# A hybrid decoder layer on one core: the order of one weight pair, and a new form of the last norm and its stores

## The chip, the cores and the metric

The kernel runs on one core of a Trainium2 chip. The metric is the device time of one execution in microseconds (us), the median over several runs. Before the change it is 730.70 us over three runs (730.41 to 731.08).

The core's engines work side by side, each through its own queue in order: TensorE (PE in the profile, with weight loads as PEld) multiplies into the eight PSUM banks, VectorE (DVE), ScalarE (ACT) and GpSimd (POOL) work element by element, and SyncE (SP) issues transfers, as ScalarE and GpSimd can too. An instruction waits on semaphores for the data or the buffer it needs, and everything behind it in its queue waits with it.

## The reference

One layer over x of 1024 tokens by 1024 channels. What matters here is its end:

```python
v = jax.nn.silu(layernorm(v, cln_g[l], cln_b[l]))
v = v @ pw2_w[l] + pw2_b[l]                       # 1024 x 1024, the pointwise projection
y_conv = v * jax.nn.silu(cs)
...
y = jnp.concatenate([y_conv, y_lru], axis=-1) @ w_out[l]
x = x + (1.0 + gate[:, None, :]) * y
return rmsnorm(x, final_g)                        # y * rsqrt(mean(x*x) + eps) * final_g
```

Ahead of it stand a modulated norm, a projection to 5120 channels, two depthwise convolutions, the gates and a linear recurrence. All is float32.

## The kernel before

Activations lie transposed: 128 channels on the partitions, tokens along the free dimension, eight channel tiles of 128 x 1024. A float32 product is made of three products of float32r operands, high x high, high x low, low x high, so each operand is split: ScalarE casts it to the high part, VectorE subtracts that to get the low part. A product of 128 x 512 outputs over half of the contraction (four k tiles) is twelve matmuls.

**The plan.** The program is written as a list of operations with an engine, an estimated cost, a priority (`prio`, lower first) and their operands. `Plan.order` runs a list scheduler over them and so fixes, for every engine, the order in which instructions stand in its queue. `after=` adds a predecessor for this plan only: it shapes the order and sets no semaphore. On the chip an instruction waits for its true operands and buffers alone.

**The pointwise projection `pw2`.** Its eight output tiles are made in four pairs (line 1363). A pair uses a scheme of seven block products (`pair_products`), whose first operations are kept as `ops[0]` to `ops[6]`. `pair_weights` (line 559) loads the pair's two weight tiles into two buffers of the pool `raw` (it has two), casts the first (`whi...`), casts half of the second (`hl...`), makes four combinations of halves in place with VectorE and splits those (`h12`, `l12`, `h34`, `l34`), in all two loads, four ScalarE casts and eight VectorE operations, with five tiles of the large pool (`big`, 47 buffers). The loads are planned after `last[:1]`, the first product of the pair before, and the combinations and the second cast after `last[1:]`, the fourth product of the pair before. The outputs `yc` are then split once more for the output projection (`quarters`, tiles `yh*`, `yl*`).

**The output projection.** Tile 6 first, then pairs (0, 1), (2, 3) and (4, 5); tile 7 (`OUT_Z`) runs beside the last pair. The accumulators are `fin0` to `fin7`, which start as the residual x plus the recurrent half's product. The last pair and tile 7 run over the columns in three pieces, `END` = 0 to 512, 512 to 768, 768 to 1024. For each piece `add` and `gated` add products into `fin`, and `squares` has ScalarE square them (`finsq`) and VectorE add the squares into `finss`; the squares of tile 7 go to a tile of their own, `finsqz`, in the second and third piece.

**The last norm, one call of `norm` (line 1429) a piece.** `rstd` (line 687) sums the square tiles over the partitions with TensorE, tile by tile (`finbc<-ones,finss`, then `finbc<-ones,finsqz`), takes the root on ScalarE (`sd`), the reciprocal on VectorE (`rs`), and spreads the result over the partitions with TensorE (`finbc<-ident,rs`). In the last piece it runs idle products as well (`warm_mm`, four ahead of the sums and two behind them, `WARM`), and a second spread into a bank `idle`. `norm` then copies the result to SBUF (`bc`, in every piece), and makes the eight outputs: VectorE multiplies `fin` by `final_g` and by the spread in one instruction; tiles 6 and 0 of the second and third piece, which ScalarE has scaled by `final_g` ahead, go to GpSimd. Each output has a store of its own, 256 KB in the first piece and 128 KB in the others, into `out[m*128:(m+1)*128, a:e]`, rows of 4 KB in DRAM of which 2 KB or 1 KB are written. SyncE issues them, ScalarE those of the tiles in `AP`.

Of the kernel before, what the change touches and what calls it, by code (L numbers as in the profile page):

```python
# [11 lines left out]
AF = mybir.ActivationFunctionType  # L12
ALU = mybir.AluOpType

P = 128
D = 1024
T = 1024
KT = D // P
# [19 lines left out]
END = ((0, H), (H, 768), (768, T))  # L38
# [18 lines left out]
WPW = ("DVE", "DVE", "DVE", "DVE")  # L57
WOUT = ("DVE", "DVE", "DVE")
WZ = "DVE"
AP = {0: (), 512: (1, 5), 768: (1, 3, 5, 7)}  # L60
NP = {0: (), 512: (6, 0), 768: (6, 0)}
SUMS = (2, 6, 1, 4, 3, 0, 7, 5)
QRES = 0
AHEAD = 4
IDLE, IDLE0 = 13, 4
WARM = (4, 2)
BEHIND = 2.6
Z0 = 0.6
ROOTP = 57
# [226 lines left out]
def hymba_layer(ctx: ExitStack, tc: tile.TileContext, xT, vecs, mod_w, w_first, w_in,  # L296
# [98 lines left out]
    def big_buf(name, dt=F32, parts=1):  # L395
        return S.buf("big", name, dt, parts)

    def bank(name):
        return S.buf("bank", name)
# [5 lines left out]
    def part(b, a, e):  # L405
        if isinstance(b, Two):
            z = a // H
            return part(b.b[z], a - z * H, e - z * H)
        return lambda: b()[:, a:e]

    def halves(b, a, e):
        if isinstance(b, Two):
            return [(b.b[z], 0) for z in (0, 1) if z * H < e and a < z * H + H]
        return [(b, i) for i in range(b.parts) if i * (T // b.parts) < e
                and a < (i + 1) * (T // b.parts)]
# [7 lines left out]
    def vec(name, t):  # L423
        o = OFF[name] + t
        return V[:, o:o + 1]
# [261 lines left out]
    def rstd(prio, sqs, a, e, ps, o, after=(), warm=(), idle=None):  # L687


        nb = (e - a) // P  # L690
        sd, rs = S.buf("sd", f"sd{prio}_{o}"), S.buf("rs", f"rs{prio}_{o}")
        wk = halves(ps, 0, e - a)


        def warm_mm():
            pe.matmul(half(idle, 0)()[:, :P], ones, ones, start=True, stop=True)

        def stats(sq, off, k):
            for b in range(nb):
                c = a - off + b * P  # L700
                pe.matmul(part(ps, b, b + 1)(), sq()[:, c:c + P],
                          ones[:, 0:1], start=k == 0 and b == 0, stop=k == len(sqs) - 1,
                          skip_group_check=True)

        def spread(ps=ps):
            for b in range(nb):
                pe.matmul(part(ps, b * P, b * P + P)(),
                          rs()[:, b:b + 1].to_broadcast([P, P]), ident, start=b % 4 == 0,
                          stop=True, skip_group_check=True)
        for _ in range(warm[0] if warm else 0):  # L710
            S.op("PE", 0.22, warm_mm, prio, [], [idle], after=enders[-2:], columns=4 * P)
        for k, (sq, off) in enumerate(sqs):
            at = S.op("PE", 0.18 * nb, lambda sq=sq, k=k, off=off: stats(sq, off, k), prio,
                      halves(sq, a - off, e - off), wk,
                      after=after if k == 0 else [])
        for _ in range(warm[1] if warm else 0):
            S.op("PE", 0.22, warm_mm, prio, [], [idle], after=[at], columns=4 * P)
        ACT(prio, lambda: sd()[:, :nb], part(ps, 0, nb), AF.Sqrt, nb, bias=eps_t,
            scale=1.0 / D, r=wk, w=[sd])
        S.op("DVE", 0.2, lambda: dve.reciprocal(rs()[:, :nb], sd()[:, :nb]), prio, [sd], [rs])  # L720
        op = S.op("PE", 0.22 * nb, spread, prio, [rs], wk, columns=4 * P * nb)
        if idle:
            S.op("PE", 0.22 * nb, lambda: spread(idle), prio, [rs], [idle], after=[op],
                 columns=4 * P * nb)
        return wk, op


# [634 lines left out]
    begun_pw2, last = [], [started[n - 1], started[n]]  # L1362
    for p in range(KT // 2):
        n = C0 + 2 * p
        w = pair_weights("pw2", p, n, last[:1], last[1:], WPW[p])
        ops, ps = next(pair_products(f"pw2_{p}", n, w, v_sets))
        begun_pw2.append(ops)
        last = [ops[0], ops[3]]
        ts, bs, ss = [], [], []
        for m in (2 * p, 2 * p + 1):  # L1370
            t, sr = big_buf(f"yc{m}", parts=2), big_buf(f"scsr{m}", parts=2)
            DMA(n - 0.5, sr, lambda m=m: scs_d[m], FULL_BYTES, r=[("scsd", m)], w=[sr],
                after=[ops[1]])
            ts.append(t)
            bs.append(vec("pw2_b", m))
            ss.append(sr)
        yc += ts
        for i, a, z, (src, *more) in ps:
            t, sr, b = ts[i], ss[i], bs[i]
            to, sg, tk, sk = part(t, a, z), part(sr, a, z), halves(t, a, z), halves(sr, a, z)  # L1380
            if more:
                STT(n + 1, to, src[0], b, more[0][0], ALU.add, ALU.add, H,
                    r=src[1] + more[0][1], w=tk)
                TT(n + 1, "DVE", to, to, sg, ALU.mult, H, r=tk + sk, w=tk)
            else:
                STT(n + 1, to, src[0], b, sg, ALU.add, ALU.mult, H, r=src[1] + sk, w=tk)
# [3 lines left out]
    y_sets = quarters(C0 + 6.5, yc, "y", True, [[begun_pw2[p][i]] for p, i in QGATES])  # L1390
    acc, n = {}, D0
    ss, qz = big_buf("finss", parts=4), big_buf("finsqz", parts=4)

    def out_acc(m, n, after, pool="big"):
        t = S.buf(pool, f"fin{m}", F32, 4)
# [30 lines left out]

    firm, enders = [], []

    def norm(n, a, e):
        w_ = e - a  # L1430
        bc = bank(f"finbc{a}")
        b2 = bank("idle") if e == T else bc
        rstd(n, [(ss, 0), (qz, 0)] if a else [(ss, 0)], a, e, bc, 0, warm=WARM if e == T else (), idle=b2 if e == T else None)
        bs = big_buf(f"bc{a}")
        for m in NP[a]:
            ACT(n + 0.2, part(acc[m], a, e), part(acc[m], a, e), AF.Copy, w_,
                scale=vec("final_g", m), r=halves(acc[m], a, e), w=halves(acc[m], a, e))
        ACT(n + 0.2, part(bs, 0, w_), part(b2, 0, w_), "copy", w_, r=[b2], w=[bs])
        for m in (*NP[a], *(i for i in range(KT) if i not in NP[a])):
            o, t = big_buf(f"o{a}_{m}"), acc[m]  # L1440
            if m in NP[a]:
                TT(D0 + 20, "POOL", part(o, 0, w_), part(t, a, e), part(bs, 0, w_), ALU.mult, w_,
                   r=halves(t, a, e) + [bs], w=[o])
            else:
                STT(D0 + 20, part(o, 0, w_), part(t, a, e), vec("final_g", m), part(bc, 0, w_),
                    ALU.mult, ALU.mult, w_, r=halves(t, a, e) + [bc], w=[o], after=firm[-1:])
            store(D0 + 20, "ACT" if m in AP[a] else "SP",
                  lambda m=m, a=a, e=e: out[m * P:(m + 1) * P, a:e], part(o, 0, w_), [o],
                  P * w_ * 4)
    for m in OUT_A:  # L1450
        weights(("out", m), last[1:], n, "DVE")
        out_acc(m, n, last[1:])
# [22 lines left out]
    for i, p in enumerate(OUT_P):  # L1475
        end = i == len(OUT_P) - 1
        w = pair_weights("out", p, n, last[:1], last[1:], WOUT[i])
        if end:
            for m in OUT_Z:
                weights(("out", m), last[1:], n, WZ)  # L1480
            n += 0.1
        for m in () if end else (2 * p, 2 * p + 1):
            out_acc(m, n - 0.5, last[1:])
        behind = i == len(OUT_P) - 2
        steps = pair_products(f"out_{p}", n, w, y_sets, 0.8 * end + BEHIND * behind, i == 0,
                              ((0, H),) if behind else PIECES)
        ops, ps = next(steps)
        for m in (*OUT_Z, 2 * p, 2 * p + 1) if end else ():
            out_acc(m, n - 0.5, [ops[1]], "big" if m in OUT_Z else "raw")
        if end:  # L1490
            last_tiles(n + Z0, 0, H)
        for z, a, e, parts in ps:
            o = add(2 * p + z, n + 1, a, e, parts)
            if end:
                firm[:] = [o]
                squares(2 * p + z, n + 1, a, e)
        last = [ops[0], ops[3]]
        if not end:
            for m in (2 * p, 2 * p + 1):
                squares(m, n + 1.5, 0, H if behind else T)  # L1500
            if behind:
                ops, ps = next(steps)
                for z, a, e, parts in ps:
                    add(2 * p + z, n + BEHIND + 0.9, a, e, parts)
                    squares(2 * p + z, n + BEHIND + 0.9, a, e)
            n += 2
    norm(n + 0.7, 0, H)
    for a, e in END[1:]:
        ops, ps = next(steps)
        for z, a, e, parts in ps:  # L1510
            firm.append(add(2 * p + z, n + 0.9, a, e, parts))
            squares(2 * p + z, n + 0.9, a, e)
        last_tiles(n + 1.1, a, e)
        n += 1
        norm(n + 0.6, a, e)
    S.run()


# [51 lines left out]
```

## Time and profile before

| | |
|---|---|
| median of three runs | 730.70 us (730.41 to 731.08) |
| the profiled execution: time, span | 730.84 us, 729.1 us |
| granted TensorE clock | 0.999 |
| TensorE busy | 720.9 us, 99% of the span |
| VectorE, ScalarE, GpSimd busy | 638.9, 460.1, 97.4 us |
| TensorE's last matmul begins | 722.3 us |
| first store of the output issued, last one issued | 711.2, 725.4 us |

The profile is one execution. Its rows name an engine, the line, the operation and its tiles (output<-inputs, with buffer numbers left out), the start and duration in us, and in square brackets the idle time of the engine just before and what ended it. Lines 338, 346, 357 and 365 are helpers that record all casts and copies, activations, fused multiply-adds and two-operand operations, so rows are told apart by their tiles. A window row has, for each engine, busy time and instructions, then the granted clock, the share of the 16 DMA engines and GB/s. Durations of following instructions on one engine overlap a little, since the next one starts before the last results are out.

### The profile page before, as it was taken

What the parts mean: (1) busy time and instruction counts of PE and PEld (TensorE: products, weight loads), DVE (VectorE), ACT (ScalarE), POOL (GpSimd) and SP (SyncE); (2) the same over time, 40 slices, a digit from 0 to 9 for tenths busy, and PEclk for the clock granted to TensorE, in tenths of its full rate; (3) what the DMA queues carried; (4) which work ended last, traced back from release to release, by engine and by line L of the source; (5) the groups of instructions that cost most, each with busy time, mean ns of one, the idle gap of its engine ahead of it and who ended that gap; (6) DMA issues with size and microseconds to landing.
All of it is one profiled execution on the core that took longest, in us unless ns stands there. A gap on an engine that the chain in (4) does not pass through costs nothing.

```text
span 729.1 us, 8918 instructions
## 1 busy us (share of the span) xinstructions
PE 720.9 (99%) x3270; PEld 600.2 (82%) x3270; DVE 638.9 (88%) x912; ACT 460.1 (63%) x619; POOL 97.4 (13%) x107
## 2 busy tenths in 40 slices
PE   9999999999999999999999999999999999999996
PEld 8888888888888888888888888888888888887886
DVE  6989999999999988688899995998999657899647
ACT  6660485777778887957867895835754334657421
POOL 0042012121221332233120100000000000000001
PEclk9999999999999999999999999999999999999999
DMA  8971024397699799599884536344223430622306
GB/s 321 407 260 75 1 73 115 94 203 172 158 252 229 147 217 235 127 220 217 181 175 86 122 78 187 102 158 169 105 102 118 171 116 0 231 80 94 116 1 231
DMA packets 37500, 112.11 MB, mean 154 GB/s; under 512 B 4168, under 2 KB 12880, under 8 KB 37456
## 3 DMA queue, kind: packets, MB, share of 16 engines
q1 hardware_dynamic: 24048, 76.50, 29.7%
q0 software_dynamic: 12528, 34.26, 26.1%
q10 hardware_dynamic: 880, 0.79, 0.3%
q8 instruction: 25, 0.41, 0.2%
q14 instruction: 19, 0.16, 0.1%
HBM read 64.69 MB, written 12.59 MB: 106 GB/s over the span
## 4 chain that ended last, share of the span: by engine, by line
PE 98%; DVE 1%; ACT 0%; issue 0%; DVEq 0%
PE ps L497 66%; PE first L777 5%; PE pbpw L608 3%; PE pupw L608 3%; PE papw L608 3%; PE gate L1201 3%; PE puout L608 2%; PE paout L608 2%; PE out L678 2%; PE pcpw L608 1%; PE pb0out L608 1%; PE pcout L608 1%; DVE o L357 1%; PE out6b L678 1%; PE late L777 1%; PE token_stats L743 1%
## 5 line engine op out<-in xcount | busy, mean ns | idle before, releaser
L497 PE MATMUL ps<-uh,whi 128*128 128x512 f32 x576 | 224.2, 389 | 0.0
L497 PE MATMUL ps<-ul,whi 128*128 128x512 f32 x576 | 224.1, 389 | 0.0
L497 PE MATMUL ps<-uh,wlo 128*128 128x512 f32 x576 | 224.1, 389 | 0.0
L497 PEld LDWEIGHTS ps<-uh,wlo 128*128 128x128 f32 x576 | 108.1, 188 | 22.6
L497 PEld LDWEIGHTS ps<-uh,whi 128*128 128x128 f32 x576 | 108.1, 188 | 22.3
L497 PEld LDWEIGHTS ps<-ul,whi 128*128 128x128 f32 x576 | 108.2, 188 | 22.3
L338 ACT CAST whi<-raw 128x1024 fp32r<-128x1024 f32 x46 | 48.1, 1047 | 38.5 <-PE ps L497 32.0
L370 POOL DMA_DIRECT2D es<-cq x45 | 40.1, 903 | 169.0 <-ACT cq L346 131.3
L346 ACT ACT_TABLE_LOAD x47 | 60.3, 1283 | 3.3 <-issue 1.5
L365 DVE TENSOR_TENSOR wlo<-raw,whi 128x1024 fp32r<-128x1024 f32 x39 | 47.5, 1219 | 13.8 <-ACT whi L338 13.6
L357 DVE SCALAR_TENSOR_TENSOR cacc<-v,V,cacc 128x511 f32<-128x511 f32 (+14 forms) x75 | 55.6, 742 | 0.6
L357 DVE SCALAR_TENSOR_TENSOR caccs<-v,V,caccs 128x511 f32<-128x511 f32 (+6 forms) x70 | 52.1, 744 | 2.2 <-ACT caccs L346 1.0
L357 DVE SCALAR_TENSOR_TENSOR caccs<-c,wsum,caccs 128x511 f32<-128x511 f32 (+6 forms) x70 | 52.0, 743 | 0.6
L497 PE MATMUL ps<-yh,whi 128*128 128x512 f32 x128 | 49.8, 389 | 0.0
L497 PE MATMUL ps<-yl,whi 128*128 128x512 f32 x128 | 49.8, 389 | 0.0
L497 PE MATMUL ps<-yh,wlo 128*128 128x512 f32 x128 | 49.8, 389 | 0.0
L370 POOL DMA_DIRECT2D oo<-co x42 | 38.3, 911 | 79.8 <-ACT co L346 32.6
L365 POOL TENSOR_TENSOR o<-fin,bc 128x256 f32<-128x256 f32 x4 | 2.8, 731 | 282.6 <-ACT bc L338 277.5
L357 DVE SCALAR_TENSOR_TENSOR xs<-ps,V,xs 128x512 f32<-128x512 f32 (+3 forms) x48 | 35.7, 745 | 0.4 <-ACT xs L346 0.2
L346 ACT ACTIVATE cq<-v,V 128x511 f32<-128x511 f32 (+14 forms) x45 | 31.9, 708 | 0.0
L357 DVE SCALAR_TENSOR_TENSOR modw<-modw,sc 128x1024 f32<-128x1024 f32 x23 | 30.0, 1313 | 0.2 <-DMA modw<-in_mod_w_dram 0.2
L346 ACT ACTIVATE cq<-c,wsum 128x512 f32<-128x512 f32 x42 | 29.6, 713 | 0.0
(380 smaller groups left out, 1445.3 us busy)
## 6 DMA issues: line engine op xcount, KB each, us to landing
raw<-in_w_in_dram SPq DMA_DIRECT2D x36, 512.0 KB, 5.3
modw<-in_mod_w_dram SPq DMA_DIRECT2D x24, 512.0 KB, 8.9
raw<-in_w_out_dram SPq DMA_DIRECT2D x10, 512.0 KB, 3.6
scsd<-scs SPq DMA_DIRECT2D x8, 512.0 KB, 4.6
acc<-in_xT_dram SPq DMA_DIRECT2D x8, 512.0 KB, 4.3
accd<-acc SPq DMA_DIRECT2D x8, 512.0 KB, 2.7
rawpw<-in_pw_dram SPq DMA_DIRECT2D x8, 512.0 KB, 3.3
scsr<-scsd SPq DMA_DIRECT2D x8, 512.0 KB, 5.6
```

Source lines behind the costliest of these rows:

```text
L338: act.copy(out(), in_())
L346: act.activation(out=out(), in_=in_(), func=func, **kw)
L357: dve.scalar_tensor_tensor(out=out(), in0=in0(), scalar=scalar, in1=in1(), op0=op0, op1=op1, accum_out=accum)
L365: lambda: e.tensor_tensor(out=out(), in0=a(), in1=b(), op=op), prio, r, w,
L370: return S.op("POOL", ISSUE, lambda: pool.dma_start(out(), a(), accum_op=ALU.add), prio, r, w, lag=RATE * n / T, after=after)
L497: pe.matmul(part(ps, a - off, b - off)(), k3(lhs)()[:, k, :], rhs[k]()[:, a:b], start=(k == 0 and lhs is wh and rhs is xh and (a - off) % ...
L608: pe.matmul(part(ps, 0, c1 - c0)(), half(*lhs)()[:, j * P:j * P + P], half(*rhs)()[:, c0:c1], start=start and j == 0 and z == 0, stop=j == ...
L678: pe.matmul(part(ps, a - off, e - off)(), k3(lhs)()[:, k, :], rhs()[:, i * H + a % H:i * H + a % H + e - a], start=k == KORD[0] and lhs is ...
L743: pe.matmul(psb()[:, :P], ones, ones, start=True, stop=True)
L777: pe.matmul(part(ps, a - off, b - off)(), fw_part(lhs, k, i * P, i * P + P)(), rhs()[:, a:b], start=k == 0 and lhs is wh and rhs is xh, st ...
L1201: pe.matmul(ps(), lhs()[:, j, :], rhs()[:, c0:c1], start=st == 0, stop=st == 2)
```

## The change

Four things change.

First, `PWE` gives the fourth `pw2` pair (p = 3) other predecessors in the plan: its loads after the last product of the second pair (`begun_pw2[1][6]`) and its combinations after the first product of the third (`begun_pw2[2][0]`).

Second, the sums of the last norm. In the third piece the squares of the last pair's even tile (4) go to a tile of their own, `finsqy`, which TensorE sums apart. The pair's tiles are taken odd first (`REV`). Of the idle products one now follows each of the first two sums and two the third. The second spread and the bank copy behind it go.

Third, the outputs. In the first piece the copy `bc` goes, and VectorE makes the eight outputs as before. In the other two ScalarE first writes `fin * final_g` of all eight tiles into two tiles `fg`, side by side in `OUT_ORDER`; when the spread is there, one VectorE or GpSimd instruction multiplies one or two neighbouring tiles in place by it (`UNITS`): four units of two tiles in the second piece, of which GpSimd takes the first two, and two single tiles and three pairs in the third, all on VectorE. The units of the second piece are recorded after the third piece's additions, and so planned behind the last of those on VectorE.

Fourth, the stores. A unit is stored in one piece of DRAM, row by row as it lies in SBUF: 256 KB for two tiles, 128 KB for one; the host puts the tiles in their places. ScalarE issues units 1 and 3 of the third piece, SyncE all others.

```diff
-AP = {0: (), 512: (1, 5), 768: (1, 3, 5, 7)}
-NP = {0: (), 512: (6, 0), 768: (6, 0)}
+AP = {512: (), 768: (1, 3)}
+UNITS = {512: ((0, 2), (2, 2), (4, 2), (6, 2)),
+         768: ((0, 1), (1, 1), (2, 2), (4, 2), (6, 2))}
+BYPOOL = {512: (0, 1), 768: ()}
+PWE = ((None, None), (None, None), (None, None), ((2, 6), (1, 0)))
+REV = -1
+OUT_ORDER = (0, 1, 2, 3, 6, 5, 4, 7)
-WARM = (4, 2)
+WARM = (1, 2)
...
-        for _ in range(warm[0] if warm else 0):
-            S.op("PE", 0.22, warm_mm, prio, [], [idle], after=enders[-2:], columns=4 * P)
         for k, (sq, off) in enumerate(sqs):
             at = S.op("PE", 0.18 * nb, lambda sq=sq, k=k, off=off: stats(sq, off, k), prio,
...
+            for _ in range(warm[0] if warm and k < len(sqs) - 1 else 0):
+                S.op("PE", 0.22, warm_mm, prio, [], [idle], after=enders[-2:], columns=4 * P)
...
-        if idle:
-            S.op("PE", 0.22 * nb, lambda: spread(idle), prio, [rs], [idle], after=[op],
-                 columns=4 * P * nb)
...
-        w = pair_weights("pw2", p, n, last[:1], last[1:], WPW[p])
+        early, later = PWE[p] if p else (None, None)
+        w = pair_weights("pw2", p, n, last[:1] if early is None else [begun_pw2[p - early[0]][early[1]]],
+                         last[1:] if later is None else [begun_pw2[p - later[0]][later[1]]], WPW[p])
...
+    flat_out = out.rearrange("d t -> (d t)")
+
-    def norm(n, a, e):
+    def norm(n, a, e, hold=None):
         w_ = e - a
         bc = bank(f"finbc{a}")
...
+        if w_ > 256:
+            for m in range(KT):
+                o, t = big_buf(f"o{a}_{m}"), acc[m]
                 STT(D0 + 20, part(o, 0, w_), part(t, a, e), vec("final_g", m), part(bc, 0, w_),
                     ALU.mult, ALU.mult, w_, r=halves(t, a, e) + [bc], w=[o], after=firm[-1:])
...
+            return None
+        bs = big_buf(f"bc{a}") if BYPOOL[a] else None
+        gain = [big_buf(f"fg{a}_{j}", parts=4) for j in (0, 1)]
+        for s, m in enumerate(OUT_ORDER):
+            ACT(n + 0.2, part(gain[s // 4], s % 4 * w_, s % 4 * w_ + w_), part(acc[m], a, e), AF.Copy,
+                w_, scale=vec("final_g", m), r=halves(acc[m], a, e), w=[(gain[s // 4], s % 4)],
+                after=[hold] if m not in (2 * OUT_P[-1], 2 * OUT_P[-1] + 1, *OUT_Z) else [])
+        if bs:
+            ACT(n + 0.2, part(bs, 0, w_), part(bc, 0, w_), "copy", w_, r=[bc], w=[bs])
+        def units():
+            for i, (s, k) in enumerate(UNITS[a]):
+                b, o = gain[s // 4], s % 4 * w_
+                pooled = i in BYPOOL[a]
+                by, keys = bs if pooled else bc, [(b, s % 4 + j) for j in range(k)]
+                unit = part(b, o, o + k * w_)
+                rows = lambda unit=unit, k=k: unit().rearrange("p (t q) -> p t q", t=k)
+                TT(D0 + 20, "POOL" if pooled else "DVE", rows, rows,
+                   lambda by=by, k=k: by()[:, :w_].unsqueeze(1).to_broadcast([P, k, w_]), ALU.mult,
+                   k * w_, r=keys + [by], w=keys, after=[] if pooled else firm[-1:])
+                at = (a * KT + s * w_) * P
+                store(D0 + 20, "ACT" if i in AP[a] else "SP",
+                      lambda at=at, k=k: flat_out[at:at + P * k * w_].rearrange("(p q) -> p q", p=P),
+                      unit, keys, P * k * w_ * 4)
+        return units
...
-                firm[:] = [o]
+                firm[:], hold = [o], o
...
+    late = []
     for a, e in END[1:]:
         ops, ps = next(steps)
-        for z, a, e, parts in ps:
+        for z, a, e, parts in ps[::REV]:
             firm.append(add(2 * p + z, n + 0.9, a, e, parts))
-            squares(2 * p + z, n + 0.9, a, e)
+            squares(2 * p + z, n + 0.9, a, e, qy if e == T and z == 0 else None)
         last_tiles(n + 1.1, a, e)
         n += 1
-        norm(n + 0.6, a, e)
+        for units in late:
+            units()
+        late = [norm(n + 0.6, a, e, hold)]
+    late[0]()
     S.run()
```

More of the change, by code (lines that the diff above doesn't have):

```diff
@@ L703, in stats, with spread @@
                           skip_group_check=True)
-        def spread(ps=ps):
+        def spread():
             for b in range(nb):
@@ L1392, in hymba_layer @@
     ss, qz = big_buf("finss", parts=4), big_buf("finsqz", parts=4)
+    qy = big_buf("finsqy", parts=4)
     def out_acc(m, n, after, pool="big"):
@@ L1427, in hymba_layer @@
     firm, enders = [], []
-    def norm(n, a, e):
+    flat_out = out.rearrange("d t -> (d t)")
+    def norm(n, a, e, hold=None):
         w_ = e - a
         bc = bank(f"finbc{a}")
[L1432 to L1444, printed above, removed]
+        rstd(n, [(ss, 0), *([(qy, 0)] if e == T else []), *([(qz, 0)] if a else [])], a, e, bc, 0, warm=WARM if e == T else (), idle=bank("idle") if e == T else None)
+        if w_ > 256:
+            for m in range(KT):
+                o, t = big_buf(f"o{a}_{m}"), acc[m]
@@ L1445, in norm @@
                 STT(D0 + 20, part(o, 0, w_), part(t, a, e), vec("final_g", m), part(bc, 0, w_),
                     ALU.mult, ALU.mult, w_, r=halves(t, a, e) + [bc], w=[o], after=firm[-1:])
-            store(D0 + 20, "ACT" if m in AP[a] else "SP",
-                  lambda m=m, a=a, e=e: out[m * P:(m + 1) * P, a:e], part(o, 0, w_), [o],
-                  P * w_ * 4)
+                at = (a * KT + m * w_) * P
+                store(D0 + 20, "SP",
+                      lambda at=at: flat_out[at:at + P * w_].rearrange("(p q) -> p q", p=P),
+                      part(o, 0, w_), [o], P * w_ * 4)
@@ L1568 @@
     r = _run(nc, [arrays], core_ids=[0])
-    return np.ascontiguousarray(r.results[0]["out_0_dram"].T)[None]
+    flat, out = r.results[0]["out_0_dram"].reshape(-1), np.empty((D, T), np.float32)
+    for a, e in END:
+        w_, order = e - a, range(KT) if e - a > 256 else OUT_ORDER
+        units = [(s, 1) for s in range(KT)] if w_ > 256 else UNITS[a]
+        for s, k in units:
+            at = (a * KT + s * w_) * P
+            rows = flat[at:at + P * k * w_].reshape(P, k, w_)
+            for j in range(k):
+                m = order[s + j]
+                out[m * P:(m + 1) * P, a:e] = rows[:, j]
+    return np.ascontiguousarray(out.T)[None]
```

## The prediction

> **What bounds the kernel now.** I read the page first, then the list of waits on TensorE, then the chain of waits through the last 100 us, and last the rows of the final 25 us engine by engine, with the DMA share in half-microsecond windows.
>
> ```profile
> span 729.1 us, 8918 instructions
> PE 720.9 (99%) x3270; PEld 600.2 (82%) x3270; DVE 638.9 (88%) x912; ACT 460.1 (63%) x619; POOL 97.4 (13%) x107
> ```
>
> The matrix engine works for 720.9 of 729.1 us, so before the last few microseconds only its idle time can be won. Its waits inside the program are short:
>
> ```profile
> PE puout L608 <- ACT eout L338: 0.7, 1, 0.7
> PE finbc L701 <- DVE finss L365: 0.2, 1, 0.2
> ```
>
> The first lies at 659.6, among the first output pair; the second at 713.2, in the last pair. So the edit on the weights can win at most 0.7, and the rest of the change plays behind the last matmul, where the chain of waits reads:
>
> ```profile
> 709.80 0.59 ACT bc L338
> 710.40 0.03 issue
> 710.42 1.41 DVE o L357 x2
> ...
> 719.33 0.39 DVE fin L357
> 719.72 0.33 DVE finss L365
> 720.06 1.56 DVE o L357 x4
> 721.62 0.11 DVE rs63.7_0_5894 L720
> 721.73 0.04 issue
> 721.77 0.72 PE finbc L707 x4
> 722.50 0.03 issue
> 722.52 0.48 DVE o L357
> ```
>
> The reader is to see three things. The first output of the first half waits for the copy `bc`, which nothing reads in that stage (`NP[0]` is empty). The square sum of the last columns goes through two VectorE additions and then a reciprocal. And only at 722.52 can the last quarter's eight outputs begin; from there they and their stores are all that is left:
>
> ```profile
> 717.00:718.00 1.00, 1.00 (x10) 1.00 (x10) 1.00 (x3) 0.00 (x0) 1.00 (x2) 1.00 1.03 385
> ...
> 723.00:724.00 1.00, 0.00 (x0) 0.00 (x0) 1.00 (x4) 0.34 (x1) 0.53 (x1) 1.00 0.11 36
> 724.00:725.00 1.00, 0.00 (x0) 0.00 (x0) 0.96 (x3) 0.00 (x0) 0.88 (x2) 1.00 1.00 327
> 726.50:727.00 0.50, 0.00 (x0) 0.00 (x0) 0.00 (x0) 0.00 (x0) 0.00 (x0) 0.98 0.96 330
> 727.00:727.50 0.50, 0.00 (x0) 0.00 (x0) 0.00 (x0) 0.00 (x0) 0.00 (x0) 0.50 0.14 45
> ```
>
> The last two figures are DMA share and GB/s. At 723 the queues are nearly empty (0.11): earlier stores are not in the way. The last 1.05 MB then flow at full rate from 724.0 to about 727.05, and 2.05 us later the span ends. That tail I keep as it is.
>
> **Part 1, the fourth weight pair.** Its two loads, four ScalarE casts and eight VectorE operations are planned against the second and third pair's products. These bindings set places in the engines' queues, no semaphore.
>
> ```profile
> 591.72 2.74 SPq L386 DMA_DIRECT2D rawpw<-in_pw_dram  x2
> 599.74 0.57 ACT L338 COPY pupw<-papw 128x512 f32<-128x512 f32 x1 [7.59 <-PE papw L608]
> 602.42 2.72 PE pupw L608 x12
> 605.66 0.62 ACT L338 CAST hlpw<-rawpw 128x512 fp32r<-128x512 f32 x1
> 611.89 1.21 DVE L365 TENSOR_TENSOR l34pw<-rawpw,h34pw 128x1024 fp32r<-128x1024 f32 x1
> 616.02 2.72 PE papw L608 x12
> 627.69 1.22 DVE L365 TENSOR_TENSOR ylb<-yc,yhb 128x1024 fp32r<-128x1024 f32 x1 [2.33 <-PE pupw L608]
> ```
>
> The loads already leave at 591.72, as soon as the two `raw` buffers are free (the later binding did not hold them), so SyncE gains nothing; behind them in its queue stand only the `scsr` loads, in the same order as now. POOL has nothing there. On ScalarE `hlpw` stands behind an evacuation at 605; it can move up some 4 us, and the last split on VectorE from 611.89 to about 607. The pair's products begin at 616.02, 2.9 us after the split ends now: nothing waits, so nothing is won there. If a cast is put in front of the copy at 599.74, that copy ends 1.05 later, at 601.4, still before the product at 602.42 that overwrites its accumulation: cost nothing, with 1.0 us of cover. What could be won is the 0.7 us at 659.6, if the splits of `y` came earlier. But VectorE stands idle for 2.33 us at 627.69 until TensorE lets go of a buffer, and is full from there to 674; work brought forward before 627 ends in that hole. I take 0, bounds -0.7 and +2.7 (one product of 12 matmuls later, as a rival below).
>
> **Part 2, the first half's outputs.** The copy `bc` goes. The outputs can then start at 709.8, where the copy starts now, instead of 710.42, 0.6 earlier. The square sums behind them move too, and TensorE's wait of 0.2 at 713.2 goes: every later matmul, and the end of the last tile, 0.2 earlier.
>
> **Part 3, the last sums.** Rows of now:
>
> ```profile
> 718.99 1.06 PE L696 MATMUL idle<-ones 128*128 128x128 f32 x8
> 720.11 0.61 PE L701 MATMUL finbc<-ones,finss 128*128 128x1 f32 x4
> 720.58 0.58 PE L701 MATMUL finbc<-ones,finsqz 128*128 128x1 f32 x4
> 719.75 0.42 ACT L346 ACTIVATE finsqz<-fin 128x256 f32<-128x256 f32 x1 [1.09 <-DVE fin L357]
> 721.26 0.26 ACT L346 ACTIVATE sd63.7_0_5888<-finbc,eps_t 128x2 f32<-128x2 f32 x1 [1.09 <-PE finbc L701]
> ```
>
> `finsqz` is there at 720.17, but its sum runs at 720.58, since `finss` comes first and waits for the addition that ends at 720.06. With the even tile's squares in `finsqy`, no late addition is left. TensorE now does: sum `ss`, one idle product, sum `qy`, one idle product, sum `qz`. Sum to sum is 0.47 (720.11 to 720.58), an idle product a quarter of 1.06, 0.26. From the last tile's end at 718.99 - 0.2 = 718.8: 0.47 + 0.26 + 0.47 + 0.26 = 1.46, so `qz` starts at 720.25; its square is ready at 719.97. Gain 720.58 - 720.25 = 0.33, bounds 0.1 (the wait at 713 stays) and 0.6 (idle products overlap the sums). The extra sum is in this; the mirrored spread that goes stood behind the real one and cost nothing. VectorE must be free for the reciprocal: between the last addition and it now lie a `finss` addition (0.33) and four outputs (1.56), later two 512-wide units. At most 2 x 0.71 = 1.42 (row below) from 719.5 ends at 720.9, and the reciprocal is due at 721.62 - 0.33 = 721.3: free. The first output of the last quarter then starts at 722.52 - 0.33 = 722.2.
>
> **Part 4, outputs by scaled copies.** ScalarE gets 16 scaled copies in place of 4, and VectorE multiplies tile pairs.
>
> ```profile
> L346 ACT ACTIVATE fin<-fin,V 128x256 f32<-128x256 f32 x4 | 1.9, 506 | 0.0
> L357 DVE SCALAR_TENSOR_TENSOR o<-fin,V,finbc 128x512 f32<-128x512 f32 x8 | 5.7, 740 | 0.5 <-ACT bc L338 0.5
> L365 DVE TENSOR_TENSOR c<-c,mean 128x512 f32<-128x512 f32 x16 | 10.1, 678 | 0.0
> 722.52 2.44 DVE L357 SCALAR_TENSOR_TENSOR o<-fin,V,finbc 128x256 f32<-128x256 f32 x6 [0.80 <-PE finbc L707]
> 723.47 1.41 POOL L365 TENSOR_TENSOR o<-fin,bc 128x256 f32<-128x256 f32 x2 [5.15 <-issue]
> 725.42 0.41 SPq L392 DMA_DIRECT2D out_dram<-o  x1
> out_dram<-o SPq DMA_DIRECT2D x8, 256.0 KB, 2.1
> out_dram<-o SPq DMA_DIRECT2D x10, 128.0 KB, 2.5
> ```
>
> The copies are 16 x 0.5 = 8 us on an engine that has gaps from 705 to 721; ten of them may run from 705 on, and of the last quarter only tiles 4 and 7 come late. If tile 7's copy follows its square at 720.0, ScalarE is free at 720.5; the square root is due at 721.26 - 0.33 = 720.9. Cost 0; without that cover 0.5 a copy.
>
> In the quarter before, two 512-wide units go to GpSimd: twice now's 2 x 0.7, so from 716.9 to 719.7, and their stores follow well before 722. In the last quarter GpSimd has none. VectorE does two units of 256 and three of 512. The row with a PSUM operand gives 10.1 / 16 = 0.63 per 512; for 256 the chain's addition gives 0.33. Sum 2 x 0.33 + 3 x 0.63 = 2.55, with the last one's drain 2.6; bounds: by the present outputs' rows (2.44 / 6 = 0.41 and 5.7 / 8 = 0.71) 2.95. So the last unit ends at 722.2 + 2.6 = 724.8, against 722.52 + 2.44 = 724.96. Its store then leaves at once, at 724.85, since five stores on two queues replace eight; now the last leaves at 725.42, behind others on SyncE's queue. That is 0.57 earlier, but it carries 256 KB in place of 128 KB, 0.38 more at 345 GB/s. And by rate: the first store leaves 0.33 earlier and 1.05 MB still take 3.05 us. The end so comes 0.2 to 0.4 earlier; I take 0.3, with 0.35 lost again at the upper bound of 2.95, and another 0.3 won if wider rows in one piece of DRAM flow at 385 instead of 345 GB/s (the window from 717 to 718 above, with 2 KB rows, shows 385).
>
> [...]
>
> **Sum.** 0 (part 1), and 0.3 at the end for parts 2 to 4, which share one path. The profiled execution took 730.84 with a span of 729.1; it comes to 730.5. That execution lies 0.14 above the median of the three runs, 730.70, so I forecast 730.4.
>
> **Rivals.**
> (B) The hole at 627.69 closes, the wait of 0.7 at 659.6 goes, and the tail takes its upper bounds (0.6 at the sum, 0.3 by rate): 730.7 - 1.6 = 729.1. For it: TensorE waits there for splits of `y` alone, and VectorE is freed some 4 us earlier. Against: the hole itself is a buffer wait that the edit does not touch.
> (C) ScalarE's queue: if the plan puts the copies of tiles 5, 4 and 7 between the last square and the square root, that is 1.5 us there, 0.9 of it free, so 0.6 late: 731.0, and 731.5 with another copy of 0.5 in front of the last square. For it: 8 us of new work in a queue that is served in order. Against: the plan ranks copies behind squares and root.
> (D) The other side: the fourth pair's five large buffers are taken earlier, and the splits of `y` get theirs one product later than 627.69. From 659.6 on TensorE has no other work left, so each microsecond there counts in full: 730.4 + 2.7 = 733.1. It decides as soon as VectorE's full stretch begins after 627.7. For it: that wait exists already. Against: by 611 the same buffers are held now too.
> That the binding moves nothing at all is within the forecast, as I gave it 0.
>
> **How the numbers follow.** Forecast 0.48, B 0.27, C 0.10, D 0.15. A measurement of this kernel can tell about 0.2%, 1.46 us: below 729.24 is faster, above 732.16 slower. Faster: three quarters of B, 0.20. Slower: D and the far part of C, 0.17. Within: 0.63. The forecast's own range is 729.8 to 731.0; the range from 728.7 to 732.6 takes in B and C and leaves out most of D and a little below, under 0.2.
>
> **What would show it.** Right: fourth pair's `l34pw` done by 608 with TensorE unmoved at 616.02; no wait of `finbc` on `finss`; first-half outputs starting at once behind `fin`; sum of `finsqz` about 0.3 earlier; five final products in 2.6 us; stores full rate till about 726.7. Wrong: a TensorE wait over 0.7 between 627 and 675 (D), or none there (B); the square root behind a scaled copy (C); 512-wide products over 0.7.

## The result, and the profile after

The changed kernel takes 728.8 us (median of 9 runs, 728.33 to 728.97), the kernel before 730.8 us (9 runs, 730.39 to 731.27): a ratio of 0.9974, 95% interval 0.9965 to 0.9983. It is 2.0 us faster, inside the range, 0.1 above its lower end, and on the side that was forecast as the less likely one; the point forecast was 730.4.

The profiled execution takes 728.67 us with a span of 726.8. First the list of waits on TensorE, which is to be read against the two waits of before:

```profile
PE token_stats L745 <- DVE ones L435: 1.1, 1, 1.1
PE first L779 <- ACT fhi L343: 0.2, 1, 0.2
```

Both are at the very start, where the two programs are alike (the second comes and goes from run to run). The wait on `eout` (0.7) and that on `finss` (0.2) are gone. The chain of waits now ends so (start, duration, what):

```profile
715.47 2.16 PE out L683 x18
717.63 0.34 PE finbc L706 x4
717.97 0.55 PE idle L701 x4
718.53 0.79 PE finbc L706 x8
719.31 0.55 PE idle L701 x4
719.87 0.72 PE finbc L712 x4
720.59 0.02 issue
720.62 0.42 DVE fg L370
721.04 0.33 DVEq L1594
721.37 1.79 DVE fg L370 x3
```

From the last tile's products to the spread the chain shows TensorE's rows alone; the VectorE rows that stood here before (`fin`, `finss`, four outputs) have gone from it. The two `idle` rows only fill time in which TensorE would wait for the last squares and for the root and the reciprocal, as the run without idle products shows below. The five last products run from 720.62 in 2.55 us:

```profile
720.62 2.55 DVE L370 TENSOR_TENSOR fg<-fg,finbc 128x256 f32<-128x256 f32 x5 [0.80 <-PE finbc L712]
```

The windows of the last stretch (busy time of TensorE, its weight loads, VectorE, ScalarE, GpSimd; clock; DMA share; GB/s):

```profile
721.00:722.00 1.00, 0.00 (x0) 0.00 (x0) 1.00 (x4) 0.00 (x0) 0.00 (x0) 1.00 0.11 36
722.00:723.00 1.00, 0.00 (x0) 0.00 (x0) 1.00 (x2) 0.00 (x0) 0.00 (x0) 0.79 0.86 290
723.00:724.00 1.00, 0.00 (x0) 0.00 (x0) 0.16 (x1) 0.00 (x0) 0.00 (x0) 0.50 1.03 381
724.00:724.50 0.50, 0.00 (x0) 0.00 (x0) 0.00 (x0) 0.00 (x0) 0.00 (x0) 0.50 1.04 393
```

The same picture as before, two microseconds earlier, with one difference: at full share the engines now move 381 to 393 GB/s, before 327 to 340 (the windows of one microsecond from 724 to 727).

Spans of single executions differ by up to 0.8 us in what lies ahead of the changed part, so for all that follows I count from the first product of the fourth `pw2` pair (`papw` at about 616), which both programs reach in the same order. In us from there:

| kernel | last `out` product | sum of `finsqz` | first output, last piece | DMA quiet | span's end |
|---|---|---|---|---|---|
| before | 103.01 | 104.72 | 106.66 | 111.20 | 113.24 |
| after | 101.71 | 103.09 | 104.98 | 109.28 | 111.16 |
| difference | -1.30 | -1.63 | -1.68 | -1.92 | -2.08 |

So 1.30 us are won while TensorE still multiplies, 0.33 between the last product and the last sum, 0.05 from there to the first output, 0.24 in the flow of the last 1.05 MB, and 0.16 behind it. "DMA quiet" is reckoned from the mean share of the 16 engines, so the last two parts are not sharp: in the kernel before, a trickle goes on behind it until 727.6, which the changed kernel does not have.

```profile
727.27:727.52 0.25, 0.00 (x0) 0.00 (x0) 0.00 (x0) 0.00 (x0) 0.00 (x0) 0.50 0.07 25
727.52:727.77 0.25, 0.00 (x0) 0.00 (x0) 0.00 (x0) 0.00 (x0) 0.00 (x0) 0.50 0.03 8
```

A share of 0.07 is about one engine of 16. The run with contiguous stores below has this trickle too, the one without the `bc` copy has not.

### The profile page after: what moved, and what is told of

Read it like the earlier page. It is cut to its first block, busy times and chain, and to the rows that moved or that the text cites. A ratio compares the mean times of both kernels' runs of the same rounds, so it can differ in the third digit from the quotient of the medians.

```text
span 726.8 us, 8902 instructions
## 1 busy us (share of the span) xinstructions
PE 719.3 (99%) x3266; PEld 599.0 (82%) x3266; DVE 638.5 (88%) x906; ACT 464.1 (64%) x629; POOL 97.3 (13%) x105
## 4 chain that ended last, share of the span: by engine, by line
PE 98%; DMA 1%; DVE 0%; SPq 0%; ACT 0%; DVEq 0%; issue 0%
PE ps L502 66%; PE first L779 5%; PE pbpw L613 3%; PE pupw L613 3%; PE papw L613 3%; PE gate L1203 3%; PE out L683 2%; PE puout L613 2%; PE paout L613 2%; PE pcpw L613 1%; PE pcout L613 1%; PE pb0out L613 1%; DMA fraw<-in_w_first_dram 1%; PE out6b L683 1%; PE late L779 1%; PE pb1out L613 0%
## 5 line engine op out<-in xcount | busy, mean ns | idle before, releaser
L370 POOL TENSOR_TENSOR fg<-fg,bc 128x512 f32<-128x512 f32 x2 | 2.5, 1290 | 276.1 <-ACT bc L343 276.1
```

The source lines that it names most:

```text
L370: lambda: e.tensor_tensor(out=out(), in0=a(), in1=b(), op=op), prio, r, w,
```

## The experiments

My theory after the result: the binding of the weight pair removed the first wait (part 1 was wrong to give it nothing), and the end's edits the rest. The rival: the end's edits, which change the whole plan from there backwards, also removed the wait. Nine kernels were run. Their points, counted as above:

| kernel | median, us | last `out` | `finsqz` | first output | DMA quiet | span's end |
|---|---|---|---|---|---|---|
| end alone | 729.99 | 102.53 | 103.99 | 105.79 | 110.10 | 112.00 |
| binding alone | 730.25 | 102.11 | 103.82 | 105.79 | 110.33 | 112.64 |
| before, contiguous stores | 730.89 | 103.03 | 104.74 | 106.69 | 111.22 | 113.29 |
| before, no `bc` copy | 730.26 | 102.50 | 104.47 | 106.47 | 110.99 | 112.65 |
| after, even tile in `finss` | 729.38 | 101.70 | 103.36 | 105.25 | 109.55 | 111.47 |
| after, no idle products | 728.72 | 101.75 | 103.06 | 104.96 | 109.26 | 111.15 |
| after, loads bound as before | 728.6 (one run) | 101.73 | 103.11 | 104.99 | 109.29 | 111.13 |
| after, single tiles | 729.27 | 101.74 | 103.12 | 105.00 | 109.47 | 111.65 |
| after, hole kept | 732.78 | 105.35 | 106.81 | 108.61 | 112.91 | 114.83 |

The runs of the kernel before beside them had medians of 730.84 to 730.89. Each row of points is one execution, and the medians do not always move as the points do: by the medians the end alone is worth 0.85 and the binding alone 0.59, 1.44 in sum against 2.0 for the change. The intervals are wide enough for both (0.2 to 1.5, 0 to 1.3, and 1.2 to 2.6 us). So parts below about half a microsecond rest on the rows, and not on the times.

**The end alone.** The changed kernel with the pair bound as before.

```diff
-PWE = ((None, None), (None, None), (None, None), ((2, 6), (1, 0)))
+PWE = ((None, None),) * 4
```

> The changed kernel with the fourth weight pair bound as before, so the end's edits alone. Theory (the binding closed the wait of 0.7 us at 659.6, because VectorE's additions and splits of y moved into its hole before 627.7): TensorE's wait there is back at about 0.7 us, the last l34pw ends near 613 again, and the time is 0.7 above the changed kernel's 728.8, about 729.5. Rival (the end's edits reshuffled the plan around 640 to 660 and so closed it): no wait, about 728.8.

Measured 729.99 us, 0.5 above the theory's 729.5, ratio to before 0.9989 (0.998 to 0.9997). The list of waits of this run has the old wait again, and not the second one:

```profile
PE puout L613 <- ACT eout L343: 0.7, 1, 0.7
```

The binding closed it. By the points it is worth 0.82 at the last product and 0.82 when the DMA falls quiet; the end's edits are worth 1.10 there (111.20 to 110.10).

**The binding alone.** The kernel before with `PWE` and the lines that read it.

```diff
+PWE = ((None, None), (None, None), (None, None), ((2, 6), (1, 0)))
...
-        w = pair_weights("pw2", p, n, last[:1], last[1:], WPW[p])
+        early, later = PWE[p] if p else (None, None)
+        w = pair_weights("pw2", p, n, last[:1] if early is None else [begun_pw2[p - early[0]][early[1]]],
+                         last[1:] if later is None else [begun_pw2[p - later[0]][later[1]]], WPW[p])
```

> The kernel before with the fourth pair's binding alone. Theory: the wait of 0.7 us goes, the end stays as it was, so 730.8 - 0.7 = 730.1. Rival: the wait stays and the time is 730.8.

Measured 730.25, ratio 0.9991 (0.9982 to 1.0), which by itself hardly tells it from none; the points do: 0.90 earlier at the last product, 0.87 at the DMA's end. By the points the two halves add up: 0.87 + 1.10 = 1.97 against 1.92 together. In this run the order near 713 changed as well (the list names a wait of 0.2 on `finsqz` in place of the one on `finss`), so 0.82, from the changed kernel and the end alone, is the better figure for the pair's wait.

Both are more than the 0.7 in the list. The rows of the kernel before show why (start, duration, matmul):

```profile
658.93 0.39 PE L608 MATMUL puout<-ylc,h34out 128*128 128x512 f32 x1
659.15 0.40 PE L608 MATMUL puout<-yhc,l34out 128*128 128x512 f32 x1
660.23 0.50 PE L608 MATMUL puout<-yhc,h34out 128*128 128x512 f32 x1 [0.68 <-ACT eout L338]
660.56 0.39 PE L608 MATMUL puout<-ylc,h34out 128*128 128x512 f32 x1
```

Matmuls start 0.22 to 0.23 apart but are drawn 0.39 long. The wait is counted from the drawn end at 659.55; from start to start 1.08 pass in place of 0.23, and the first matmul after it takes another 0.10 more. So a listed wait of 0.68 costs 0.85 + 0.10 = 0.95. The changed kernel has a small pause of its own a little later:

```profile
663.69 0.39 PE L613 MATMUL paout<-yha,wloout 128*128 128x512 f32 x1
663.94 0.50 PE L613 MATMUL pcout<-yhT,hlout 128*128 128x512 f32 x1
664.28 0.39 PE L613 MATMUL pcout<-ylT,hlout 128*128 128x512 f32 x1
```

By exact starts these two steps are together 0.13 longer than two usual ones of 0.227, and 0.95 - 0.13 = 0.82 is what the points gave.

How the wait went is seen in the chain of waits and in one split of VectorE, first in the kernel before, then in the changed one:

```profile
658.86 0.70 PE puout L608 x3
659.59 0.60 ACT eout L338
660.23 3.02 PE puout L608 x12
659.20 1.22 DVE L365 TENSOR_TENSOR wloout<-rawout,whiout 128x1024 fp32r<-128x1024 f32 x1
```

```profile
655.92 2.72 PE puout L613 x12
658.64 1.36 PE paout L613 x6
660.00 2.72 PE puout L613 x12
657.32 1.22 DVE L370 TENSOR_TENSOR wloout<-rawout,whiout 128x1024 fp32r<-128x1024 f32 x1
```

TensorE may write `puout` again only when ScalarE has copied it to `eout`. Before, nothing stands between the two. In the changed kernel six products of the next output pair (`paout`) do, and the copy runs beside them. Every third of them needs that pair's low weights, `wloout`, which VectorE splits right behind the last split of `y`. In the kernel before these were ready at 660.42, after the wait.

This other order on TensorE is the plan's. The kernels here that have the new place of the combinations in the plan differ from the old order from about 643 on, and those without it keep the old order until past 708. So the runs show what the binding does to the plan as a whole; early splits with TensorE's old order were not tried.

**Only the later half of the binding.** Loads as before, combinations bound to the third pair's first product.

```diff
-PWE = ((None, None), (None, None), (None, None), ((2, 6), (1, 0)))
+PWE = ((None, None), (None, None), (None, None), (None, (1, 0)))
```

> The changed kernel with the fourth pair's loads bound as before and only the combinations bound to the third pair's first product. Theory (the loads leave at about 591.7 in either case, the place of the casts and combinations in the queues does it): no wait of TensorE near 659, the last l34pw ends by 608, time as the changed kernel. Rival (the earlier loads do it): the wait of 0.7 is back.

One run: 728.6 us, every point within 0.03 of the changed kernel, no wait. The loads' place does nothing that this run shows; the place of the casts and combinations does it.

**The hole kept.** If the theory is right, taking the freed work out of VectorE's idle time must bring the wait back. `quarters` gets a further predecessor for the second half of the splits of `y`, for the plan alone:

```diff
-    def quarters(pr, xs, tag, whole=False, gates=None):
+    def quarters(pr, xs, tag, whole=False, gates=None, late=()):
...
             p += TLATE
+            g = [*g, *late]
...
-    y_sets = quarters(C0 + 6.5, yc, "y", True, [[begun_pw2[p][i]] for p, i in QGATES])
+    y_sets = quarters(C0 + 6.5, yc, "y", True, [[begun_pw2[p][i]] for p, i in QGATES], [begun_pw2[3][4]])
```

> The changed kernel, binding and end as they are, but the second half of the splits of y (the differences yu and yt and what is made of them) may be planned only after the fourth pair's fifth product has begun, at about 627, where that work mostly stood before the change. Theory (TensorE's wait near 659 went because VectorE did this work in its idle time before 627.7): VectorE is idle some 2 to 3 us before 628 again, the last ylT ends 1.5 us or more after 656.7, TensorE's wait is back with 0.5 us or more, and the time is at least 0.6 above 728.8. Rival (the earlier weights alone did it, whatever y does): no wait, 728.8.

Measured 732.78, ratio to before 1.0026 (1.0015 to 1.0037). Its TensorE waits:

```profile
PE paout L614 <- ACT puout L343: 1.7, 1, 1.7
...
PE puout L614 <- ACT eout L343: 0.7, 1, 0.7
PE puout L614 <- DVE ylc L370: 0.6, 1, 0.6
```

VectorE's busy time between 617 and 627.7, and its last split `ylT`, in the kernel before, the changed one and this one, a fence each:

```profile
617.00:627.70 10.70, 8.00 (x13) 1.00 0.42 149
658.60 0.68 DVE L365 TENSOR_TENSOR ylT<-yu,yhT 128x512 fp32r<-128x512 f32 x1
```

```profile
617.00:627.70 10.70, 9.96 (x15) 1.00 0.41 149
656.06 0.69 DVE L370 TENSOR_TENSOR ylT<-yu,yhT 128x512 fp32r<-128x512 f32 x1
```

```profile
617.00:627.70 10.70, 5.16 (x8) 1.00 0.42 149
661.34 0.68 DVE L370 TENSOR_TENSOR ylT<-yu,yhT 128x512 fp32r<-128x512 f32 x1
```

The less VectorE does before 627.7, the later its last split: 5.16, 8.00 and 9.96 us of work, `ylT` at 661.34, 658.60 and 656.06. From 627.7 to 659 it is full in all three (31.30, 31.09 and 31.26 of 31.30 us in the kernel before, the changed one and this one), so work that misses the hole pushes everything behind it, and TensorE pays once it has no other product left. This run shows the condition with the binding in place, but the direction and not the size: it leaves VectorE idle for 5.5 us of that stretch, where the theory expected 2 to 3 and the kernel before has 2.7, and ends 1.9 above the kernel before.

**Contiguous stores alone.** The kernel before; only the place of each output in DRAM differs.

```diff
+    flat_out = out.rearrange("d t -> (d t)")
...
-                  lambda m=m, a=a, e=e: out[m * P:(m + 1) * P, a:e], part(o, 0, w_), [o],
+                  lambda at=(a * KT + m * w_) * P: flat_out[at:at + P * w_].rearrange("(p q) -> p q", p=P),
+                  part(o, 0, w_), [o],
...
```

The part left out puts the tiles in their places on the host.

> The kernel before with nothing changed but where each output lies in DRAM: every store writes one contiguous piece, tile by tile, same sizes, same queues. Theory (the last 1.05 MB flow faster when contiguous, 375 in place of 345 GB/s): the DMA engines' last busy stretch is 0.25 us shorter and the time 0.2 to 0.3 below 730.8. Rival (it is the 2 KB rows of the pairs, or the queues, that make the rate): no difference.

A miss for the theory: 730.89, ratio 1.0001 (0.9993 to 1.001). The flow from the first output to the quiet DMA takes 4.53, before 4.54.

**Single tiles in the last piece.**

```diff
-         768: ((0, 1), (1, 1), (2, 2), (4, 2), (6, 2))}
+         768: tuple((s, 1) for s in range(8))}
-AP = {512: (), 768: (1, 3)}
+AP = {512: (), 768: (1, 3, 5, 7)}
```

> The changed kernel with eight single tiles in the last piece: eight products of 256, eight stores of 128 KB with rows of 1 KB, alternating between SyncE and ScalarE, each still one contiguous piece. Theory (rows of 2 KB make the last 1.05 MB flow at 375 to 385 in place of 345 GB/s): the DMA engines need 0.25 longer from the first store to the end, 729.0 to 729.1, although the first product starts at the same time. Rival (the pairs only save issues): 728.8 or less, as the products then feed more evenly.

Measured 729.27, ratio to before 0.9978 (0.9969 to 0.9987); its interval overlaps that of the changed kernel. The points tell them apart: the first output comes at the same time (105.00 and 104.98), the DMA is quiet 0.19 later, and the span ends 0.49 later. Its windows at full share:

```profile
723.00:724.00 1.00, 0.00 (x0) 0.00 (x0) 0.59 (x2) 0.00 (x0) 0.00 (x0) 0.50 1.04 340
724.00:724.50 0.50, 0.00 (x0) 0.00 (x0) 0.00 (x0) 0.00 (x0) 0.00 (x0) 0.50 1.02 336
```

Contiguous pieces with rows of 1 KB flow at 336 to 342 GB/s, about as the strided ones did (327 to 340). It is the row of 2 KB that flows at 381 to 393, not the layout in DRAM. The size of a store changes with the row here (128 and 256 KB), but the trace has a record for each row: in the last piece of the changed kernel, where both kinds flow together, a row of 1 KB takes 48.6 ns on average (256 records) and one of 2 KB 86.6 (384 records), so two narrow rows cost 97.

**No `bc` copy in the first piece.** The kernel before, otherwise unchanged.

```diff
-        bs = big_buf(f"bc{a}")
+        bs = big_buf(f"bc{a}") if NP[a] else None
...
-        ACT(n + 0.2, part(bs, 0, w_), part(b2, 0, w_), "copy", w_, r=[b2], w=[bs])
+        if bs:
+            ACT(n + 0.2, part(bs, 0, w_), part(b2, 0, w_), "copy", w_, r=[b2], w=[bs])
```

> The kernel before without the copy of the spread to SBUF in the first piece, which nothing reads there. Theory: the first outputs start about 0.6 earlier, at 709.8, TensorE's wait of 0.2 on finss near 713 goes, and the end comes 0.2 earlier: 730.6. Rival (VectorE's later additions wait for TensorE and ScalarE anyway): 730.8.

Measured 730.26, ratio 0.999 (0.9981 to 0.9999). The last product comes 0.51 earlier, but the first output of the last piece only 0.19 and the quiet DMA 0.21: TensorE's sum then waits for the addition into `finss` (from the last product to the sum of `finsqz` 1.97, before 1.71). The span's end, however, comes 0.59 earlier and the median 0.58: this execution lacks the trickle that the kernel before has behind the quiet DMA. That the copy's removal pays in full only with the sums apart is so by the points up to the quiet DMA, and not shown by the times.

**The even tile back in `finss`.**

```diff
-        rstd(n, [(ss, 0), *([(qy, 0)] if e == T else []), *([(qz, 0)] if a else [])], ...
+        rstd(n, [(ss, 0), *([(qz, 0)] if a else [])], ...
...
-            squares(2 * p + z, n + 0.9, a, e, qy if e == T and z == 0 else None)
+            squares(2 * p + z, n + 0.9, a, e, None)
```

> The changed kernel with the even tile's squares added into finss again, so two sums in place of three. In the changed kernel the sum of finsqz starts 1.10 us after the last tile's products, before the change 1.59. Theory (the sum was late because TensorE waited for the last VectorE addition into finss): it starts 1.4 to 1.6 after them again, and the first output and the end come 0.3 to 0.5 later, 729.2. Rival (fewer outputs on VectorE made the addition early enough, the separate tile adds nothing): unchanged or 0.2 earlier, since one sum of 0.34 is saved.

Measured 729.38, ratio 0.9982 (0.9973 to 0.9991). The sum starts 1.66 after the last product in place of 1.38, and the first output and the quiet DMA come 0.27 later (the median 0.58). The chain names the reason:

```profile
717.66 0.48 DVE fin L362
718.14 0.34 DVE finss L370
718.48 0.04 issue
718.53 1.05 PE finbc L706 x8
```

The addition into `finss` is ordered behind tile 7's, and both sums wait for it.

**No idle products.** `WARM = (0, 0)`.

> The changed kernel without the four idle products among the last sums. Theory (they only fill time while TensorE waits for finsqz, and delay it by at most one of 0.27): the sum of finsqz starts up to 0.25 earlier and the spread keeps its 0.72, so 728.6 to 728.8. Rival (they keep the clock up): the granted clock falls before the spread, which takes 1.4, and the time is 729.5.

Measured 728.72, ratio to before 0.9974 (0.9963 to 0.9985), no difference to the changed kernel, and the points agree within 0.04. The sum of `finsqz` now waits for its squares, which end at 718.36:

```profile
718.41 0.61 PE L706 MATMUL finbc<-ones,finsqz 128*128 128x1 f32 x4 [0.24 <-ACT finsqz L351]
719.56 0.71 PE L712 MATMUL finbc<-ident,rs63.7_0_5887 128*128 128x128 f32 x4 [0.55 <-DVE rs63.7_0_5887 L725]
```

The spread takes 0.71 with waits of 0.24 and 0.55 before it, so the idle products neither delay nor help. The granted clock reads 1.00 in the windows up to 722 of this run, past the spread, 0.69 in the one from 722 to 723 and 0.50 from 723 on. The spread ends at 720.27, and a window at 0.69 means that the fall to half came at about 722.4, some 2.1 us later (an estimate from these windows). So the clock did not fall before the spread.

## Why the prediction was right or wrong

**Part 1 failed, and with it the likeliest case.** The step was "work brought forward before 627 ends in that hole". The hole of 2.33 us at 627.69 was a wait for a buffer by one instruction, `ylb`, and I took it for a wall. Other splits of `y` needed no buffer that was late. With the weights' last split at 606.52 in place of 611.89, the plan put them there, the last split of `y` and `wloout` behind it came 2.3 and 1.7 us earlier (counted from the fourth pair's first product), and TensorE had six products of the next pair to run while ScalarE copied `eout`. Rival B said that the hole closes, and gave 729.1 for it; that case came (728.8). Its reason was only half right: TensorE's listed wait is for the copy `eout`, not for a split of `y`. And that its number came so close is in part luck, since its 0.6 at the sum was about 0.3 there, made up by 0.48 at the last product. The rest of part 1 holds: the loads left when the buffers were free, moving them did nothing, and no cast delayed other work (the first one ran at 594.95, in idle time of ScalarE, and the copy of `papw` starts 16.12 ahead of the fourth pair in both kernels).

**A size was off by the way waits are drawn.** I priced the wait near 659 at its listed 0.7 and that at 713 at 0.2. From start to start they cost 0.95 and, at 713, 0.49 less a pitch of 0.12, 0.37. The binding measured 0.82 to 0.90; at the last product the end's edits won 0.48, where part 2 gave 0.2. Of the 0.48, 0.11 stay untraced.

**Part 2 was right in mechanism.** The outputs of the first piece start 0.6 sooner behind the spread, and `finbc` no longer waits for `finss`. Counted from the fourth pair they start 0.32 earlier (94.57 to 94.25), since the new plan has the spread 0.3 later; the run without the copy alone has the whole 0.60. That part of the gain is lost again while the last sum hangs on VectorE was not foreseen; in the change both come together.

**Part 3 was right.** From the last product to the sum of `finsqz` 0.33 are won (1.71 to 1.38); of the forecast's 0.33, though, 0.2 was the earlier last product. Taken alone the separate sum is worth 0.27. The plan put two idle products behind the first sum and none behind the second, which changes nothing.

**Part 4 was right in its feed and missed the rate as the likely value.** The five products took 2.55, the sum that I took. ScalarE took its copies without a delay (C did not come): before the root it waits 0.35 for TensorE's sum. The rate I left at 345 as the value and 385 as a bound; it was 381 to 393, worth 0.24. I had guessed "wider rows in one piece of DRAM": the rows alone do it, and the first pieces of the kernel before, strided rows of 2 KB, already showed it (385 GB/s, 86.9 ns a row).

**The sum** was 0.3 for parts 2 to 4, and so too small by 0.8. They measured 1.10 at the DMA's end: 0.48 at the last product, 0.25 from there to the sum, 0.14 to the first output, 0.23 in the flow. The case of the other side, D, did not come: taking buffers earlier delayed no split.

What stays open: 0.16 between the quiet DMA and the end of the span. That stretch lies between 1.66 and 2.31 us in these single executions and follows no edit. The trickle does not account for it: counted from the last row stored it still lies between 1.4 and 2.1. Why the trickle comes in some executions was not found.

## What to carry to other kernels

An engine's idle time in front of a full stretch is worth looking at by instruction: what waits there may be one buffer (2.33 us of VectorE before `ylb` here), and other work of the same stretch may fit in. Price a TensorE wait by the distance between matmul starts, not by the listed idle time (0.95 against 0.68 here). And where a final reduction ends the kernel, take the last terms straight to the matrix engine in tiles of their own (0.27 here) and let stores of wide rows follow (381 to 393 GB/s with rows of 2 KB, 327 to 342 with rows of 1 KB); an edit that makes only one of two parallel paths earlier can lose part of its gain where they join (0.51 became 0.19 here).

## What the runs showed of the hardware that was not expected

In the windows at full DMA share (0.99 to 1.04) the stores from SBUF to DRAM flowed by the row they read and write, not by the layout. With rows of 1 KB: 327 to 340 GB/s strided (last piece of the kernel before), 331 to 342 contiguous (the runs with contiguous stores and with single tiles). With rows of 2 KB: 381 to 393 contiguous (last piece of the changed kernel; 377 to 379 in the end alone), 385 strided (first piece of the kernel before).

In the kernel before, a VectorE addition of 128x512 with one operand in PSUM took no longer than one from SBUF: 678 ns for `c<-c,mean` (mean of 16), 689 for the additions into `finss` (mean of 7).
